# The opening of a two-layer encoder: order of the first loads, PSUM banks for two blocks of x, idle products, place of the squares, and a new table of places

## Chip, core and metric

The kernel runs on one core of one Trainium2 chip. The metric is the device time of one execution in microseconds (us). Within a core, TensorE (PE; its weight loads are shown apart as PEld), VectorE (DVE), ScalarE (ACT), GpSimd (POOL) and SyncE (SP) each run their own queue of instructions in order and wait for each other through semaphores. [...]

## What is computed

Two layers of an encoder on x, 256 rows of 1024 columns, in float32. Each layer has a mixer (three kinds of attention side by side) and a channel part:

```python
for l in range(DEPTH):
    x = mixer_sublayer(x, ...)       # rms_norm, h @ w_in, three attentions, rms_norm each, @ w_out, + x
    x = channel_sublayer(x, ...)     # rms_norm, @ w_gate_up, conv over rows, gelu(g) * u, @ w_down, + x
```

For the opening, this is what matters: the first thing computed is `rms_norm(x, norm1_g[0]) @ w_in[0]`, with `w_in[0]` 1024 by 2560. The kernel multiplies by the gain `norm1_g` first, leaves the division by the root mean square for later, and so needs the sums of the squares of x only where the first results are used.

## The kernel before

**Products in three.** Every operand is split into a large and a small part (`hi`, `lo`), and a product of full precision is three matmuls: hi by hi, hi by lo, lo by hi (`mm3`, line 708). The `hi` of weights is made by an ACT copy and the `lo` by a DVE subtraction, piece by piece (`split`, lines 676 to 695); for the first two units of weights a piece is one block of 128 rows by 384 columns.

**Units of weights.** The weights come in units of up to 1 MB into four raw buffers, and are split into two pairs of `hi` and `lo` buffers. A unit of the first projection is four blocks of 128 rows by 384 columns; the first projection, `dq`, takes unit 0 (blocks 0 to 3 of x) and unit 1 (blocks 4 to 7), for two halves of the rows, t = 0 and 1: 24 matmuls per unit. `dk` takes units 2 and 3, `dv` units 4 and 5, and so on.

**Opening.** `START` (line 45) lists the first transfers by queue: x in five pieces (a pair is first block and number of blocks), the gains `g`, the identity `ident`, and the four blocks `w` of unit 0. `LANDS` (line 52) has the time, in ns, at which the planner takes each of them to have landed. `split_T` (line 722) transposes x on PE, block by block: two blocks, each for t = 0 and 1, share one PSUM tile of a bank; ACT then writes `hi`, times the gain, into hT, and DVE the `lo`. `mean_squares` (line 746) has ACT square x in four pieces (two halves of the columns, two of the rows) with sums; POOL makes the root mean square of them. Before all that, PE runs idle products on a tile of ones (`warm`, `WARM` and `WARM_MORE`, lines 577 to 590): 13 of them at their place, and 15 more with a rank 1000 later, which the planner puts wherever PE would otherwise have nothing to do.

**Order.** No engine's order is written by hand. The program is first recorded as a list of operations (`Plan.add`), numbered as they come, and then put in order by a planner (`Plan.order`, line 323): at every step it takes the operation that can start first by its own costs (`cost`, line 475), its due times and its free buffers; among those that can start at the same time, the one with the smallest rank. A rank is the operation's number, plus what `later` adds, plus an entry of the table `PLACES` (line 229), by number. PSUM counts as one region for a whole bank (`footprint`, line 137), so a reader of one half waits for the writers of the other. `nc.behind` names an operation that must come first; it is a further dependency of what is recorded while it is set.

The attention's chain, which the steps touch: dq's and dk's sums of squares on ACT, their root on POOL (`small_ms`, `small_rstd`), scaling and rotation on DVE (`act_z`, `act_sw`), transposes on PE. POOL also repeats the bias table (`na_repeat`, line 829: `act_nab<-act_few`). Projections are the work that PE does beside that (`Weave`).

Of the kernel before, what the change touches and what calls it, by code (L numbers as in the profile page):

```python
# [11 lines left out]
F32 = mybir.dt.float32  # L12
F32R = mybir.dt.float32r
I32 = mybir.dt.int32
AF = mybir.ActivationFunctionType
# [29 lines left out]
START = [  # L45
    ("act", "x", (0, 1)), ("sync", "g", 0), ("act", "x", (1, 1)), ("sync", "ident", 0), ("sync", "w", 0),
    ("sync", "w", 1), ("sync", "x", (2, 2)), ("sync", "w", 2), ("sync", "w", 3), ("sync", "x", (4, 2)),
# [3 lines left out]

LANDS = (4100, 3300, 5300, 3450, 5800, 6450, 7250, 8200, 8900, 9800, 10700, 10750, 10800)


WARM, WARM_MORE, WARM_W = 13, 15, 256

# [168 lines left out]
def handover(a, b):  # L225
# [3 lines left out]
PLACES = {  # L229
# [6 lines left out]
}  # L236
# [281 lines left out]
def encoder_kernel(  # L518
# [102 lines left out]
    views = [v for l in range(DEPTH) for v in units_of(l)]  # L621
    raws, parts, taken = [], [], [0]

# [52 lines left out]
    def split(i):  # L676
# [13 lines left out]
        for c in range(0, n if i not in kept else 0, h):  # L690
            e = min(c + h, n)
            nc.scalar.copy(hi[:, c:e], raw[:, c:e])
            nc.vector.tensor_tensor(lo[:, c:e], raw[:, c:e], hi[:, c:e].bitcast(F32), op=ALU.subtract)
        r = lambda z: z[:, :n].rearrange("p (a b) -> p a b", b=b)
# [27 lines left out]
    def split_T(srcs, hi, lo, k0, g, name):  # L722


        n = g.shape[1]
        for b in range(0, n, 2):
            m = min(2, n - b)
            ps = psw.tile([P, 2, S], F32, tag="w", name=f"pt_{name}_{b}")
            for i in range(m):
                k = b + i  # L730
                for t in range(NT):
                    nc.tensor.transpose(
                        ps[:, i, t * P : (t + 1) * P], srcs[t][:, k * P : (k + 1) * P], ident
                    )
            for i in range(m):
                k = b + i
                h, o = hi[:, k0 + k], lo[:, k0 + k]
                nc.scalar.activation(h, ps[:, i], AF.Copy, scale=g[:, k : k + 1])
                nc.vector.scalar_tensor_tensor(
                    o, ps[:, i], g[:, k : k + 1], h.bitcast(F32), ALU.mult, ALU.subtract  # L740
                )
# [4 lines left out]
    def mean_squares(name):  # L746

        ss = small.tile([P, NT, 2], F32, tag="ssx", name=f"ssx_{name}", bufs=2)
        for h in range(2):
            for t in range(NT):  # L750
                junk = act.tile([P, 512], F32, tag="s2k", name=f"sq_{name}{t}{h}", bufs=NS2K)
                nc.scalar.activation(
                    junk, xs[:, t, h * 512 : (h + 1) * 512], AF.Square, accum_out=ss[:, t, h : h + 1]
                )
        s1 = small.tile([P, NT], F32, tag="s1x", name=f"s1_{name}", bufs=2)
        nc.gpsimd.tensor_tensor(s1, ss[:, :, 0], ss[:, :, 1], op=ALU.add)
# [795 lines left out]
```

## Time and profile before

| | us |
|---|---|
| median of three runs | 608.26 (607.88 to 608.92) |
| profiled execution | 608.41 |
| its span | 606.6 |
| PE busy in the span | 600.9 |
| ACT busy | 428.6 |
| DVE busy | 484.9 |

The span runs from the first to the last instruction that the profile shows; what lies around it is the start and the end of the program. Almost all instructions are issued through one line, 472, so the profile's groups are told apart by tiles: `const_warm` is the idle products, `const_x` x, `wp_raw`, `wp_hi` and `wp_lo` the weights as loaded and split, `act_hT` the transposed x, `act_s2k` among others the squares, `psa_a` and `psw_w` PSUM. In a timeline, a row has the start, the time (of all instructions of the row, where an xcount is over 1), the engine, what is written and read, and in brackets the idle time of the engine before it with what ended it. Matmuls are pipelined, so the distance of their starts says more than their durations.

### The profile page before, as it was taken

The page shows a single profiled execution, that of the slowest core. Times are in us where ns is not written, and L with a number is a line of the kernel's source. Part 1 is how long each engine was busy: PE and PEld are TensorE (multiplying, and loading weights), DVE is VectorE, ACT ScalarE, POOL GpSimd, SP SyncE. Part 2 cuts the span into 40 slices and gives each one's busy share as a digit, 9 for nine tenths or more (in the row PEclk, how much of TensorE's full clock was granted, in tenths as well). Part 3 has the DMA queues.
Part 4 walks back from the last instruction along what each step waited for, and adds up shares of the span by engine and source line. Part 5 has one row for each costly group of instructions (what it writes and reads, how often), then busy time and mean ns, then how long its engine had stood idle before and what let it go on. Part 6 is the DMA issues. An engine that isn't in the chain of part 4 may idle for free.

```text
span 606.6 us, 9899 instructions
## 1 busy us (share of the span) xinstructions
PE 600.9 (99%) x3496; PEld 526.7 (87%) x3496; DVE 484.9 (80%) x995; ACT 428.6 (71%) x1065; POOL 80.9 (13%) x130
## 2 busy tenths in 40 slices
PE   8999999999999999999999999999999999999997
PEld 7999898888888888888899989888888888888886
DVE  4899897997788988887777898777977777777775
ACT  6889999686666767666688899676765555665661
POOL 2733030103400000000022214421000000000000
PEclk9999999999999999999999999999999999999999
DMA  8994303566598899988455726844465555555601
GB/s 280 296 294 140 105 36 107 195 202 228 185 224 297 278 342 322 318 304 290 153 147 162 248 70 243 291 163 139 142 205 209 174 175 206 184 166 207 199 9 69
DMA packets 85217, 121.44 MB, mean 200 GB/s; under 512 B 9880, under 2 KB 69880, under 8 KB 85168
## 3 DMA queue, kind: packets, MB, share of 16 engines
q1 hardware_dynamic: 82896, 112.17, 56.3%
q0 software_dynamic: 1728, 8.39, 3.9%
q8 instruction: 27, 0.44, 0.3%
q10 hardware_dynamic: 544, 0.26, 0.2%
q14 instruction: 22, 0.18, 0.1%
HBM read 110.93 MB, written 9.88 MB: 199 GB/s over the span
## 4 chain that ended last, share of the span: by engine, by line
PE 96%; ACT 2%; DVE 1%; POOL 0%; issue 0%; DVEq 0%; ACTq 0%; POOLq 0%
PE psw_w L472 53%; PE psa_a L472 43%; ACT act_s2k L472 1%; ACT wp_hi L472 0%; DVE act_z L472 0%; DVE wp_lo L472 0%; POOL small_rstd L472 0%; ACT act_z L472 0%; ACT act_hT L472 0%; DVE act_sw L472 0%; POOL small_ms L472 0%; DVE const_x L472 0%; DVE act_qo L472 0%; POOL const_warm L472 0%; DVEq L472 0%
## 5 line engine op out<-in xcount | busy, mean ns | idle before, releaser
L472 DVE TENSOR_TENSOR wp_lo<-wp_raw,wp_hi 128x512 fp32r<-128x512 f32 (+2 forms) x332 | 231.5, 731 | 59.1 <-ACT wp_hi L472 39.3
L472 ACT CAST wp_hi<-wp_raw 128x512 fp32r<-128x512 f32 (+2 forms) x332 | 203.0, 663 | 22.8 <-PE psw_w L472 10.2
L472 PE MATMUL psw_w<-act_hT,wp_hi 128*128 128x512 f32 x704 | 180.4, 393 | 0.0
L472 PEld LDWEIGHTS psw_w<-act_hT,wp_hi 128*128 128x128 f32 x704 | 127.8, 189 | 24.8 <-DVE act_hT L472 0.7
L472 PE MATMUL psa_a<-wp_hi,act_hT 128*128 128x384 f32 (+2 forms) x448 | 113.1, 333 | 0.7 <-ACT wp_hi L472 0.7
L472 PEld LDWEIGHTS psw_w<-act_hT,wp_lo 128*128 128x128 f32 x704 | 97.7, 190 | 6.8
L472 PE MATMUL psw_w<-act_hT,wp_lo 128*128 128x256 f32 x704 | 102.2, 282 | 0.0
L472 PEld LDWEIGHTS psa_a<-wp_hi,act_hT 128*128 128x128 f32 x448 | 78.3, 189 | 3.4 <-ACT wp_hi L472 0.9
L472 ACT COPY act_s2k<-psw_w 128x256 f32<-128x256 f32 x88 | 32.4, 373 | 62.2 <-PE psw_w L472 61.9
L472 PE MATMUL psa_a<-wp_lo,act_hT 128*128 128x384 f32 (+2 forms) x224 | 74.4, 334 | 0.1
L472 PE MATMUL psa_a<-wp_lo,act_ch 128*128 128x512 f32 (+1 forms) x176 | 68.9, 392 | 0.0
L472 PE MATMUL psa_a<-wp_hi,act_ch 128*128 128x512 f32 x176 | 68.8, 392 | 0.0
L472 PE MATMUL psa_a<-wp_hi,act_cl 128*128 128x512 f32 (+1 forms) x176 | 68.5, 393 | 0.0
L472 DVE TENSOR_TENSOR act_s2k<-psw_w,act_s2k 128x256 f32<-128x256 f32 x88 | 36.6, 421 | 14.5 <-ACT act_s2k L472 14.1
L472 PEld LDWEIGHTS psa_a<-wp_lo,act_hT 128*128 128x128 f32 x224 | 42.2, 189 | 2.4 <-DVE wp_lo L472 1.0
L472 PEld LDWEIGHTS psa_a<-wp_hi,act_cl 128*128 128x128 f32 x176 | 33.1, 188 | 7.5
L472 PEld LDWEIGHTS psa_a<-wp_hi,act_ch 128*128 128x128 f32 x176 | 33.2, 189 | 6.7
L472 PEld LDWEIGHTS psa_a<-wp_lo,act_ch 128*128 128x128 f32 x176 | 33.1, 188 | 6.7
L472 DVE SCALAR_TENSOR_TENSOR act_s2k<-act_s2k,act_cw,act_s2k 128x255 f32<-128x255 f32 x88 | 36.7, 477 | 1.4 <-ACT act_s2k L472 1.3
L472 ACT ACTIVATE act_s2k<-act_s2k 128x512 f32<-128x512 f32 x22 | 13.9, 631 | 30.2 <-DVE act_s2k L472 30.2
L472 ACT ACTIVATE act_s2k<-act_s2k,act_cw 128x256 f32<-128x256 f32 x44 | 24.1, 595 | 15.3 <-DVE act_s2k L472 15.3
L472 POOL TENSOR_TENSOR small_rstd<-small_ms,const_mh 128x6 f32<-128x6 f32 (+2 forms) x26 | 30.8, 1186 | 14.4 <-DVE small_ms L472 12.8
(132 smaller groups left out, 791.6 us busy)
## 6 DMA issues: line engine op xcount, KB each, us to landing
wp_raw<-in_w_gate_up_dram SPq DMA_DIRECT2D x44, 1024.0 KB, 5.1
wp_raw<-in_w_down_dram SPq DMA_DIRECT2D x22, 1024.0 KB, 7.3
wp_raw<-in_w_in_dram SPq DMA_DIRECT2D x14, 768.0 KB, 6.0
wp_raw<-in_w_in_dram SPq DMA_DIRECT2D x8, 1024.0 KB, 9.1
wp_raw<-in_w_out_dram SPq DMA_DIRECT2D x8, 768.0 KB, 8.4
dram_khi<-act_mixT_hi SPq DMA_DIRECT2D x4, 768.0 KB, 3.6
dram_klo<-act_mixT_lo SPq DMA_DIRECT2D x4, 768.0 KB, 8.3
wp_lo<-dram_klo POOLq DMA_DIRECT2D x4, 768.0 KB, 4.8
```

The source lines that it names most:

```text
L472: getattr(o.engine.real, o.method)(*map(real, o.args), **{k: real(v) for k, v in o.kw.items()})
```

## The change

- **Loads.** Unit 0's first block of weights goes on ACT's queue as its second transfer, and x's second block goes on SP's queue in its place. `LANDS` is set anew.
- **A bank each.** Blocks 0 and 1 of x in layer 0 (`ALONE`) get a PSUM tile each instead of sharing one.
- **Idle products.** `WARM_MORE` is 7 instead of 15.
- **Squares.** In layer 0 the squares of x's first half of the columns (`HELD`) depend on the last ACT cast of unit 0.
- **Other order.** `PLACES` has 75 entries instead of 56. As there are eight idle products fewer, number n of the new table is number n + 8 of the old. So read, 47 entries are the same, nine old ones are gone and 28 are new. Seventeen of the new ones lie between the new numbers 67 and 320: later by some 100 are one transpose of x's block 5, the evacuation of block 7 and the last square; earlier are the first two casts of unit 1 (85 and 87), the transpose of the other gains (158), four of dq's sums of squares with POOL's two steps behind them (181 to 187) and POOL's repeat of the bias table (300); one of dk's scalings (274) is later, and three PE instructions move by 20 to 83. The other eleven new ones are casts of weights, a scaling, a square and five up-projection matmuls in later stages of both layers.

```diff
 START = [
-    ("act", "x", (0, 1)), ("sync", "g", 0), ("act", "x", (1, 1)), ("sync", "ident", 0), ("sync", "w", 0),
+    ("act", "x", (0, 1)), ("sync", "g", 0), ("act", "w", 0), ("sync", "ident", 0), ("sync", "x", (1, 1)),
     ("sync", "w", 1), ("sync", "x", (2, 2)), ("sync", "w", 2), ("sync", "w", 3), ("sync", "x", (4, 2)),
...
-LANDS = (4100, 3300, 5300, 3450, 5800, 6450, 7250, 8200, 8900, 9800, 10700, 10750, 10800)
+LANDS = (4100, 3300, 4800, 3800, 5200, 5900, 6900, 7700, 8500, 9400, 10400, 10500, 10600)
+ALONE = ("n100",)
+HELD = (("n10", 0),)
-WARM, WARM_MORE, WARM_W = 13, 15, 256
+WARM, WARM_MORE, WARM_W = 13, 7, 256
...
 PLACES = {
+    67: 104, 79: 101, 85: -246, 87: -158, 117: 90, 158: -74, 181: -210, 182: -210, 184: -212, 185: -212, 186: -212,
+    187: -212, 237: 20, 274: 315, 300: -116, 315: 83, 320: 49, 520: -53, 542: 173, 583: -96, 586: 125, 608: -286,
...
             nc.scalar.copy(hi[:, c:e], raw[:, c:e])
+            if i == 0:
+                split_at[:] = [len(nc.ops) - 1]
...
-            ps = psw.tile([P, 2, S], F32, tag="w", name=f"pt_{name}_{b}")
+            if name in ALONE and b == 0:
+                ps = [psw.tile([P, S], F32, tag="w", name=f"pt_{name}_{i}") for i in range(m)]
+            else:
+                both = psw.tile([P, 2, S], F32, tag="w", name=f"pt_{name}_{b}")
+                ps = [both[:, i] for i in range(m)]
...
         for h in range(2):
+            nc.behind = split_at[0] if (name, h) in HELD else None
             for t in range(NT):
                 junk = act.tile([P, 512], F32, tag="s2k", name=f"sq_{name}{t}{h}", bufs=NS2K)
...
+        nc.behind = None
```

More of the change, by code (lines that the diff above doesn't have):

```diff
@@ L621, in encoder_kernel @@
     views = [v for l in range(DEPTH) for v in units_of(l)]
-    raws, parts, taken = [], [], [0]
+    raws, parts, taken, split_at = [], [], [0], []
     PER_LAYER = len(views) // DEPTH
@@ L732, in split_T @@
                     nc.tensor.transpose(
-                        ps[:, i, t * P : (t + 1) * P], srcs[t][:, k * P : (k + 1) * P], ident
+                        ps[i][:, t * P : (t + 1) * P], srcs[t][:, k * P : (k + 1) * P], ident
                     )
@@ L737, in split_T @@
                 h, o = hi[:, k0 + k], lo[:, k0 + k]
-                nc.scalar.activation(h, ps[:, i], AF.Copy, scale=g[:, k : k + 1])
+                nc.scalar.activation(h, ps[i], AF.Copy, scale=g[:, k : k + 1])
                 nc.vector.scalar_tensor_tensor(
-                    o, ps[:, i], g[:, k : k + 1], h.bitcast(F32), ALU.mult, ALU.subtract
+                    o, ps[i], g[:, k : k + 1], h.bitcast(F32), ALU.mult, ALU.subtract
                 )
```

12 rows, old and new, of the table PLACES are left out of this document.

## Prediction

> **What bounds the kernel now.** I read the page first: the busy times, then the chain that ended last.
>
> ```profile
> span 606.6 us, 9899 instructions
> PE 600.9 (99%) x3496; PEld 526.7 (87%) x3496; DVE 484.9 (80%) x995; ACT 428.6 (71%) x1065; POOL 80.9 (13%) x130
> PE 96%; ACT 2%; DVE 1%; POOL 0%; issue 0%; DVEq 0%; ACTq 0%; POOLq 0%
> ```
>
> TensorE (PE) is busy 600.9 of 606.6 us and carries 96% of the chain. The change takes no real product away, only eight idle ones, so it can win time only where PE waits, or runs idle products, for want of data. The waits of PE after 15 us, by what ended them, and the stages of the first 120 us, say where that is.
>
> ```profile
> PEld psw_w L472 <- issue: 1.4, 5, 0.4
> PEld psa_a L472 <- DVE wp_lo L472: 0.7, 2, 0.4
> PEld psw_w L472 <- ACT wp_hi L472: 0.7, 2, 0.4
> PEld psw_w L472 <- DVE act_hT L472: 0.7, 3, 0.4
> PEld psw_w L472 <- DVE wp_lo L472: 0.2, 1, 0.2
> ```
> ```profile
> 7.30:14.16 6.86, 6.17 (x40) 5.58 (x39) 5.11 (x13) 6.74 (x20) 0.29 (x2) 1.00 1.03 358
> ...
> 20.00:35.00 15.00, 14.90 (x89) 14.55 (x88) 13.24 (x32) 12.54 (x56) 14.26 (x23) 1.00 0.96 287
> 35.00:60.00 25.00, 25.00 (x180) 23.80 (x180) 24.18 (x69) 22.03 (x77) 5.77 (x10) 1.00 0.74 211
> 60.00:120.00 60.00, 60.00 (x413) 52.30 (x412) 53.48 (x136) 52.30 (x144) 10.77 (x14) 1.00 0.32 105
> ```
>
> The columns of the second fence are the stretch, its length, the busy time of PE, PEld, DVE, ACT and POOL, granted clock, DMA share and GB/s. After 15 us PE has little to win: its weight loads wait 3.7 us in all, in 13 pieces. From 7.30 to 14.16 it is ScalarE (ACT) that is full, 6.74 of 6.86 us. So the opening bounds itself: PE starts late and then waits for ACT. The opening on PE, then on ACT:
>
> ```profile
> 0.98 3.17 PE L472 MATMUL psw_w<-const_warm 128*128 128x256 bf16 x14 [0.98 <-POOL const_warm L472]
> ...
> 4.70 0.63 PE L472 MATMUL psw_w<-const_ident,const_x 128*128 128x128 f32 x2
> 5.13 1.27 PE L472 MATMUL psw_w<-const_warm 128*128 128x256 bf16 x5
> 6.19 0.54 PE L472 MATMUL psw_w<-const_ident,const_x 128*128 128x128 f32 x2
> ...
> 7.30 0.44 PE L472 MATMUL psa_a<-wp_hi,act_hT 128*128 128x384 f32 x1
> ...
> 14.16 0.61 PE L472 MATMUL psa_a<-wp_hi,act_hT 128*128 128x384 f32 x2 [0.69 <-ACT wp_hi L472]
> ```
> ```profile
> 5.66 0.51 ACT L472 CAST wp_hi<-wp_raw 128x384 fp32r<-128x384 f32 x1 [2.64 <-DMA wp_raw<-in_w_in_dram]
> 6.77 0.48 ACT L472 ACTIVATE act_hT<-psw_w,const_gains 128x256 fp32r<-128x256 f32 x1 [0.60 <-DVE wp_lo L472]
> 7.14 0.50 ACT L472 CAST wp_hi<-wp_raw 128x384 fp32r<-128x384 f32 x1
> 7.54 0.63 ACT L472 ACTIVATE act_s2k<-const_x 128x512 f32<-128x512 f32 x1
> ...
> 8.17 0.46 ACT L472 ACTIVATE act_hT<-psw_w,const_gains 128x256 fp32r<-128x256 f32 x1
> ...
> 12.26 0.83 ACT L472 ACTIVATE act_hT<-psw_w,const_gains 128x256 fp32r<-128x256 f32 x2
> ...
> 12.98 0.64 ACT L472 ACTIVATE act_s2k<-const_x 128x512 f32<-128x512 f32 x1
> ...
> 13.59 3.41 ACT L472 CAST wp_hi<-wp_raw 128x384 fp32r<-128x384 f32 x8
> ```
>
> x's first block is transposed at 4.70 to 5.33, its second at 6.19 to 6.73. ACT evacuates the first (act_hT) only at 6.77, because both share one PSUM bank, which the planner treats as one region. The first product follows at 7.30. The second unit's first product stands at 14.16, 0.69 us late, because its cast stands behind the last square of x on ACT: 12.98, then 13.59.
>
> **The change part by part.**
> *A bank for each of two blocks.* ACT can evacuate block 0 when its own transposes end, 4.70 + 0.63 = 5.33, instead of 6.77. One more PSUM buffer of four is held for a while; at this point only the idle products and the gains hold others, so I cost it at nothing.
>
> *First weights on ACT's queue, x's second block on SyncE's (SP).* Each DMA takes the other's place, so no issue is added and the bytes ahead of the third transfer are the same. How early the weights land is not shown. The ends are the landing of the one transfer ahead of them on ACT's queue and today's cast:
>
> ```profile
> const_x<-in_x_dram ACTq DMA_DIRECT2D x1, 128.0 KB, 2.3
> ```
>
> Issued at 0.72, x's first block landed at 0.72 + 2.3 = 3.0; today's weights let ACT go at 5.66. I take 4.9, nearer to 5.66, since another block of x competes with them. Little hangs on it. ACT needs 0.37 (6.77 to 7.14) for block 0 and about 0.5 for the cast, so with 5.33 as the start both are done at 6.2; with weights at 5.66 only at 6.3. What then stands ahead of the first product is PE's own order: x's second block is due (LANDS 5200) before that product, so its two transposes go first and PE is free at about 6.4 (today 6.57). **First product: 7.30 to 6.4, a lead of 0.9.**
>
> *Fewer idle products.* 28 become 20. Of today's 28, 27 run before 7.30, in time in which PE has no data; removing them wins nothing by itself, beyond letting the two transposes go some 0.2 earlier, which is in the 6.4.
>
> *Squares of x later.* Four squares stand on ACT between 7.54 and 13.59, 0.63 each (7.54 to 8.17) and 0.61 (12.98 to 13.59). The first two now wait for the fourth cast of unit 0, and by the new places the first two casts of unit 1 go ahead of ready squares. ACT's work up to unit 1's first cast, without squares, is 4 casts at 0.40 (7.14 to 7.54) and 8 evacuations at 0.36 (12.26 to 12.98 for two): 4.5 us, or 5.33 + 4.5 = 9.8. Unit 1 isn't there yet:
>
> ```profile
> wp_raw<-in_w_in_dram SPq DMA_DIRECT2D x1, 384.0 KB, 4.6
> ```
> ```profile
> 6.28 2.06 SPq L472 DMA_DIRECT2D wp_raw<-in_w_in_dram  x4
> ```
>
> Issued at 6.28 and 4.6 us under way, its first half landed at 10.9. The cast and the handover make 10.9 + 0.5 + 0.1 = 11.5 for the earliest product of unit 1 as far as ACT goes, and 1.1 us is left on ACT for one or two squares meanwhile. Behind the waiting squares nothing is queued by the hold itself; the planner puts other work ahead. Who waits for them is POOL:
>
> ```profile
> 15.32 0.40 POOL L472 TENSOR_SCALAR small_he<-small_mex 128x2 f32<-128x2 f32 x1
> 18.68 0.29 POOL L472 TENSOR_SCALAR small_ms<-small_ss,small_he 128x6 f32<-128x6 f32 x1 [2.97 <-ACT act_s2k L472]
> ```
>
> Their sum is ready 3 us before its first use, so a delay by two squares (1.25 us) is covered; without that cover each would cost 0.6.
>
> PE has to do, between its first product and unit 1, 24 products and the 12 transposes left:
>
> ```profile
> 15.39:20.08 4.69, 4.69 (x28) 1.00 1.03 310
> ```
>
> 28 products in 4.69 us are 0.17 each, so 4.1; the transposes 1.2 at about 0.1, other small things 0.2: 5.5. PE comes to unit 1 at 6.4 + 5.5 = 11.9, after ACT's 11.5. **Lead at this point: 14.16 - 11.9 = 2.2.** Above that nothing is to be had: PE would be without a gap from 6.4 on.
>
> *How much of 2.2 survives.* ACT's and DVE's work isn't less, it is reordered. ACT ends unit 1's casts and all squares at about 5.33 + 4.5 + 2.5 (squares) + 1.6 (four casts) + 0.6 (waits for x and weights) = 14.5, against 13.59 + 4 x 0.41 = 15.2 today: ACT's own lead is 0.7. What it lacks it must take from idle time later, which exists:
>
> ```profile
> 23.42 1.76 ACT L472 CAST wp_hi<-wp_raw 128x384 fp32r<-128x384 f32 x4 [1.96 <-DMA wp_raw<-in_w_in_dram]
> ```
>
> ACT sits idle 1.96 us before 23.42. With dk's product done 2 us sooner, its squares can fill that gap. Between 35 and 120 us DVE is busy 77.7 of 85 us and ACT 74.3, so neither stops a lead of 1 to 2 us but neither gives it freely. Bounds for what is kept: 0.7 (ACT's lead) and 2.2. I take the middle, **1.5**.
>
> *Other order.* Seventeen new places lie in the opening and first projections (their part is in the sum above), eleven in later stages, and nine old ones go. What they can win there is bounded by the 3.7 us of waits after 15 us, most of them pieces of 0.2 to 0.4 that weight loads ahead of time hide; what they can lose no row shows, and I bound it by one such piece. I take 0.1 gained, between -0.4 and +0.4.
>
> Sum: 1.5 + 0.1 = 1.6. The profiled execution took 608.41 us, the span 606.6 and 1.8 around it, which stays; it lies 0.15 above the median, 608.26. **Forecast 608.41 - 1.6 = 606.8.**
>
> **The rivals.**
> *ACT's lead only.* DVE and ACT keep their order and PE's lead above 0.7 turns into waits near 34 us, where it waits for wp_lo even now. For it speaks ACT's 6.74 of 6.86; against, the 1.96 idle. Time: 608.41 - 0.7 = 607.7.
>
> *Transfers pace it.* The cast at 23.42 waits for weights, and the DMA share is 1.03 and 0.96 in the stages shown above up to 35 us, so that landing can't move. If all behind it holds its time, only the wait near 34 is saved: 608.41 - 0.3 = 608.1. Against it: PE reaches those weights, three units of 24 products at 0.17 after 14.16, only at 26.4, so a lead of 2 us still finds them.
>
> *PE's slow rate lasts.* Idle products come every 0.21 us until 6.19 (five from 5.13 to 6.19) and faster later:
>
> ```profile
> 6.57 0.82 PE L472 MATMUL psw_w<-const_warm 128*128 128x256 bf16 x6
> ```
>
> six until 7.30 are 0.12 each, though the granted clock reads 1.00 throughout. So PE needed 5.4 us of unbroken work (0.98 to 6.4) for full speed. With 20 idle products there may be a gap before the first product. If the slow rate lasts until about 10, 3.4 us of products run at half speed and 1.7 is lost: 608.5. [...] Against it: PE stays busy to within some tenths of the first product.
>
> *Slower: POOL's copy in the way.* The new places move the 2.16 us copy of the bias table ahead of dk's statistics on POOL, which is busy 14.26 of 15 us in 20 to 35:
>
> ```profile
> 24.12 2.16 POOL L472 COPY act_nab<-act_few 28x1984 f32<-28x1984 f32 x1
> ...
> 26.58 0.89 POOL L472 TENSOR_SCALAR small_ms<-small_ss,small_he 128x6 f32<-128x6 f32 x1 [0.29 <-ACT act_s2k L472]
> ```
>
> Today it ends 0.3 before dk's statistics can start. If it begins less than 2.16 before they could, the whole dk chain is late by up to 2.16, and with ACT's lead alone the time is 608.41 - 0.7 + 2.16 = 609.9. It decides once that delay exceeds PE's lead. Against it: the copy needs only its own small load, and dq's statistics are moved ahead of it.
>
> **How the numbers follow.** Forecast 0.55 (606.2 to 607.1); all 2.2 and the later waits kept, 605.9, 0.06; ACT's lead only 0.17; transfers 0.10; slow rate 0.05; POOL 0.07. 0.2% is 1.2 us, about what a measurement of this kernel can tell from no change; from the median that puts "faster" below 607.05. Faster: 0.55 + 0.06 and 0.03 of the ACT case, whose lead may be larger, 0.64; same 0.29; slower 0.07. The range 605.7 to 608.5 leaves out the slower case and the tails.
>
> **What the profile after would show.** Right: ACT's first evacuation at about 5.4, ahead of the second block's transposes; first product near 6.4; unit 1's first product near 12 with no ACT wait before it; squares between unit 0's and unit 1's casts; a PE wait near 33 of not much over 0.4. Wrong: a first product after 7 (weights or order), products at twice their interval (clock), a new PE wait on wp_lo or act_z of 1 us or more between 20 and 40 (lead given back), or dk's statistics behind act_nab on POOL.

## The result and the profile after

The changed kernel takes 610.38 us (median of 18 runs, 608.68 to 611.41); the kernel before took 608.49 on the same chips (18 runs, 607.88 to 609.52). The ratio is 1.0029, interval 1.0023 to 1.0036: 0.3% **slower**, 1.9 us, where 606.8 was forecast. The profiled execution took 610.58 with a span of 608.8.

The page of the kernel after, busy times and the chain that ended last:

```profile
span 608.8 us, 9884 instructions
PE 601.8 (99%) x3488; PEld 526.5 (86%) x3488; DVE 485.3 (80%) x995; ACT 428.2 (70%) x1065; POOL 83.2 (14%) x130
PE 94%; DVE 4%; ACT 1%; POOL 1%; issue 0%; POOLq 0%; DVEq 0%; ACTq 0%
```

PE is as busy as before, and its share of the chain fell from 96 to 94%, to DVE's gain. Something besides PE has come onto the path. The timeline of ACT in the opening, after:

```profile
4.99 1.28 ACT L480 ACT_TABLE_LOAD   x1 [4.99 <-DVE const_gains L480]
6.29 0.47 ACT L480 ACTIVATE act_hT<-psw_w,const_gains 128x256 fp32r<-128x256 f32 x1
6.66 0.50 ACT L480 CAST wp_hi<-wp_raw 128x384 fp32r<-128x384 f32 x1
...
10.66 0.84 ACT L480 ACTIVATE act_hT<-psw_w,const_gains 128x256 fp32r<-128x256 f32 x2 [2.03 <-PE psw_w L480]
```

And one row of the same timeline before:

```profile
1.74 1.28 ACT L472 ACT_TABLE_LOAD   x1 [1.74 <-issue]
```

In both profiles ACT loads a function table (`ACT_TABLE_LOAD`, 1.28 us) ahead of its first instruction that computes. Before, that was a cast that waits for a transfer, and the table load ran at 1.74, when nobody needed ACT. After, the first is an evacuation, which needs the gains from DVE and the transposes from PE, and the wait for DVE stands ahead of the table load. It runs at 4.99, and block 0 is evacuated at 6.29. PE in the opening, after:

```profile
4.90 0.60 PE L480 MATMUL psw_w<-const_warm 128*128 128x256 bf16 x4
5.34 0.38 PE L480 MATMUL psw_w<-const_ident,const_x 128*128 128x128 f32 x2
7.21 0.62 PE L480 MATMUL psa_a<-wp_hi,act_hT 128*128 128x384 f32 x2 [1.49 <-ACT wp_hi L480]
7.81 0.69 PE L480 MATMUL psa_a<-wp_lo,act_hT 128*128 128x384 f32 x1
8.29 0.52 PE L480 MATMUL psa_a<-wp_hi,act_hT 128*128 128x384 f32 x1
8.61 0.52 PE L480 MATMUL psa_a<-wp_lo,act_hT 128*128 128x384 f32 x1
```

The weights came early, and x's second block is transposed at 5.34 instead of 6.19: the loads do what they should. Then PE stands still for 1.49 us until 7.21, with no idle products left to run. The products that follow are 0.32 apart instead of 0.17, and the granted clock (the last but two of the columns) says why. It is 0.50 between 8.5 and 11.0, and in stretches of 5 us:

```profile
5.00:10.00 5.00, 3.51 (x17) 2.84 (x16) 2.38 (x5) 3.44 (x6) 0.00 (x0) 0.78 0.96 322
10.00:15.00 5.00, 5.00 (x30) 4.73 (x30) 2.04 (x6) 4.33 (x13) 0.00 (x0) 0.88 1.05 372
15.00:20.00 5.00, 5.00 (x29) 4.79 (x29) 4.95 (x11) 5.00 (x20) 2.41 (x6) 1.00 1.00 299
```

The first product of unit 1 stands at 14.99, 0.8 us later than before. More is lost behind that. What PE and its weight loads waited for from 15 to 60 us, after:

```profile
PE psw_w L480 <- ACT act_s2k L480: 0.8, 1, 0.8
...
PEld psa_a L480 <- DVE wp_lo L480: 1.3, 4, 0.4
PEld psw_w L480 <- ACT act_s2k L480: 1.0, 1, 1.0
PEld psa_a L480 <- DVE act_z L480: 0.4, 1, 0.4
PEld psw_w L480 <- ACT wp_hi L480: 0.2, 1, 0.2
```

The wait of 0.8 to 1.0 us stands at 53 us and is new, as are small ones at 28, 30 and 38. The first product of the FFN, a mark behind both, in before and after:

```profile
120.14 0.50 PE L472 MATMUL psw_w<-act_hT,wp_hi 128*128 128x512 f32 x1
```
```profile
122.96 0.50 PE L480 MATMUL psw_w<-act_hT,wp_hi 128*128 128x512 f32 x1
```

It is 2.8 us late; what follows gives 0.6 of that back, and the span is 2.2 us longer. So there are two questions: what the opening lost, and what PE lost between unit 1 and the FFN.

### The profile page after: what moved, and what is told of

The parts are those of the page before. It is cut to its first block, busy times and chain, and to the rows that moved or that the text cites. A ratio compares the mean times of both kernels' runs of the same rounds, so it can differ in the third digit from the quotient of the medians.

```text
span 608.8 us, 9884 instructions
## 1 busy us (share of the span) xinstructions
PE 601.8 (99%) x3488; PEld 526.5 (86%) x3488; DVE 485.3 (80%) x995; ACT 428.2 (70%) x1065; POOL 83.2 (14%) x130
## 4 chain that ended last, share of the span: by engine, by line
PE 94%; DVE 4%; ACT 1%; POOL 1%; issue 0%; POOLq 0%; DVEq 0%; ACTq 0%
PE psw_w L480 52%; PE psa_a L480 42%; DVE wp_lo L480 2%; DVE act_z L480 1%; DVE act_sw L480 0%; POOL small_ms L480 0%; POOL small_rstd L480 0%; ACT L480 0%; DVE const_v L480 0%; ACT act_z L480 0%; DVE act_ko L480 0%; ACT act_qo L480 0%; ACT wp_hi L480 0%; DVE act_nab L480 0%; ACT act_s2k L480 0%
## 5 line engine op out<-in xcount | busy, mean ns | idle before, releaser
L480 PE MATMUL psa_a<-wp_hi,act_ch 128*128 128x512 f32 (+1 forms) x176 | 68.9, 392 | 0.0
```

Of the source, the lines that this page charges most:

```text
L480: getattr(o.engine.real, o.method)(*map(real, o.args), **{k: real(v) for k, v in o.kw.items()})
```

## The experiments

Sixteen kernels ran, one of them twice (e13 and e16). "Unit 1" is the start of unit 1's first product, "FFN" that of the FFN's first, both from the one profiled execution; "between" is their difference. Ratios are against the kernel before, run in the same rounds, with their intervals. A wait of PE that is given below with the time at which it begins is the distance between the starts of two products, less the usual 0.17.

How far marks of single executions scatter, three kernels with the same opening and order up to small moves show: before, e9 and e14 have unit 1 at 13.99 to 14.20 and the FFN at 119.95 to 120.14. An execution can also lie far off its kernel's median. e10's profiled one took 610.67, 2.3 us over the median; that excess lies behind the FFN, from where it takes 488.8 us to the end, against 486.5 before.

| kernel | median, us | ratio | unit 1 | FFN | between |
|---|---|---|---|---|---|
| before | 608.49 | 1 | 14.16 | 120.14 | 105.98 |
| after | 610.38 | 1.0029 [1.0023, 1.0036] | 14.99 | 122.96 | 107.97 |
| e1 early table | 608.42 | 1.0001 [0.9993, 1.0010] | 12.68 | 121.61 | 108.93 |
| e2 PE filled | 609.88 | 1.0023 [1.0014, 1.0031] | 13.51 | 121.66 | 108.15 |
| e4 bank alone | 608.41 | 0.9998 [0.9989, 1.0006] | 14.04 | 120.74 | 106.70 |
| e5 old places | 612.71 | 1.0063 [1.0048, 1.0079] | 15.17 | 123.91 | 108.74 |
| e6 sums in one | 609.11 | 1.0014 [1.0005, 1.0023] | 12.63 | 120.79 | 108.16 |
| e7 copy behind tables | 609.07 | 1.0012 [1.0003, 1.0021] | 12.74 | 121.09 | 108.35 |
| e8 cast first, both | 608.74 | 1.0007 [0.9997, 1.0017] | 12.63 | 120.11 | 107.48 |
| e9 before, sums apart | 608.49 | 1.0001 [0.9992, 1.0010] | 13.99 | 119.95 | 105.96 |
| e10 new opening, old order | 608.35 | 0.9998 [0.9989, 1.0007] | 12.61 | 120.15 | 107.54 |
| e11 old opening, new order | 609.92 | 1.0022 [1.0013, 1.0031] | 14.19 | 122.13 | 107.94 |
| e12 lo9 later | 608.95 | 1.0002 [0.9993, 1.0011] | 12.64 | 120.89 | 108.25 |
| e13 copy on ACT | 607.99 | 0.9987 [0.9978, 0.9995] | see e16 | see e16 | |
| e14 before, copy on ACT | 608.52 | 1.0000 [0.9990, 1.0010] | 14.20 | 119.95 | 105.75 |
| e15 short squares | 608.34 | 0.9995 [0.9986, 1.0004] | 12.55 | 119.57 | 107.02 |
| e16 copy on ACT again | 608.45 | 0.9988 [0.9978, 0.9997] | 12.83 | 120.42 | 107.59 |
| e17 late table, old order | 609.60 | 1.0013 [1.0004, 1.0021] | 13.09 | 120.32 | 107.23 |
| e18 new order, copy on ACT | 608.37 | 0.9999 [0.9990, 1.0008] | 12.61 | 120.42 | 107.81 |

### The opening: table load, clock, bank

**e1.** One column is copied on ACT ahead of its first operation, so that the table load belongs to an instruction without a wait.

```diff
             for i in self.order():
                 o = self.ops[i]
+                if o.engine.name == "ACT" and o.method != "dma_start" and self.first_act:
+                    out, src = self.first_act
+                    self.scalar.real.copy(out.bind(), src[:, :1].bind())
+                    self.first_act = None
```

> The changed kernel with one more instruction: a one-column ACT copy ahead of ACT's first evacuation, so that the load of ACT's function table (1.28 us) no longer stands behind the wait for the gains; nothing else is reordered. Theory A (the table load on the path opens a wait on PE, in which its rate falls): the table load at about 1.7, first product near 6.1 instead of 7.21, no products at half rate, unit 1 near 12, time 606.5 to 607.3. Rival B (the new places after the opening cost about 2 us by themselves): first product as early, but the waits between 28 and 54 us stay and the time is 608.5 to 609.5.

Timeline of ACT in e1:

```profile
1.74 1.28 ACT L482 ACT_TABLE_LOAD   x1 [1.74 <-issue]
3.03 0.19 ACT L482 COPY const_fo<-const_mh 128x1 f32<-128x1 f32 x1
4.99 0.47 ACT L492 ACTIVATE act_hT<-psw_w,const_gains 128x256 fp32r<-128x256 f32 x1 [1.76 <-PE psw_w L492]
```

The evacuation is at 4.99, the first product at 5.91, unit 1 at 12.68, 1.5 us ahead of before. The time falls by 2.0 us against after, to that of the kernel before. So the table load is shown to be the loss of the opening; but a lead of 1.5 us is not worth 1.5 us. The time is just below the rival's range, and the waits that the rival named have stayed. The second question is what remained.

**e2.** The changed kernel with 16 more idle products ahead of the first product; the table load stays late.

```diff
+                if o.method == "matmul" and self.first_product and o.args[0].tile is not self.first_product[1].tile:
+                    n, ps, one = self.first_product
+                    for _ in range(n):
+                        self.tensor.real.matmul(ps.rearrange(...), one.bind(), ..., start=True, stop=True)
+                    self.first_product = None
```

> The changed kernel with 16 more idle products between the second block's transposes and the first real product, so that PE doesn't stand idle there; the table load stays on the path. Theory A: first product still near 7.2, but products at 0.17 instead of 0.32 between 7 and 11; the part of the loss that the rate makes goes, about 1.2 of 2: 608.6 to 609.3. If the rate doesn't matter (ACT alone is late): 610 and over, no change from the changed kernel.

The first product stays at 7.27, the granted clock reads 1.00 from 5 us on, and unit 1 comes at 13.51, 1.5 us earlier than in after. The median is 0.5 us lower, but the intervals of e2 and after overlap. The executions of after point the same way: in 8 of the 18 the mean granted clock is 0.996 or 0.997, with a median of 610.63, and in the other ten 0.999 or 1.000, with 609.99. So in after a low clock follows PE's idle 1.5 us (0.78 from 5 to 10 us), and most of what it cost at unit 1 is not in the end time.

**e4.** The kernel before with the bank each alone.

```diff
+            if name in ALONE and b == 0:
+                ps = [psw.tile([P, S], F32, tag="w", name=f"pt_{name}_{i}") for i in range(m)]
```

> The kernel before with one part of the change, a PSUM bank each for blocks 0 and 1. Theory A: an evacuation becomes ACT's first instruction, the table load goes behind the wait for the gains (start near 4.7 instead of 1.7) and the first product comes at 6.9 to 7.3, no earlier than in the kernel before; time 608.3 to 610. Without theory A (the bank alone lets ACT start at 5.3): first product near 6.4 and time 607.3 to 608.

Its table load runs at 4.48, its first evacuation at 5.77 instead of 6.77, and the first product at 6.74. Unit 1 stays at 14.04, since ACT is full until then: it is busy 9.64 of the 10 us from 5 to 15, and PE waits 0.70 for its cast. No gain and no loss.

**e5.** The changed kernel with the old table of places, every number less 8.

```diff
-PLACES = {67: 104, 79: 101, 85: -246, ...}
+PLACES = {367: -35, 480: 15, 520: -53, ...}
```

> The changed kernel with the table of places of the kernel before, renumbered; the table load stays on the path. Theory A: no faster than the changed kernel, 610 to 611.5. Rival B (the new places are the loss): back to 608 to 609.

It is 2.3 us slower than after. Places that were set for one stream of times don't fit another: the old table is not the old order. Part of it is the clock again: in four of its six executions the mean granted clock is 0.994 to 0.997, with a median of 613.45, against 611.18 in the other two. So this run can't tell what the new order costs; e10 and e11 do.

### What PE lost behind the opening: two pairs of engines

In e1 three rows stood out, two on POOL, one on DVE (the first of the two shown):

```profile
23.87 1.98 POOL L492 COPY act_nab<-act_few 28x1984 f32<-28x1984 f32 x1
...
45.12 1.99 POOL L492 TENSOR_SCALAR small_ms<-small_ss,small_he 128x6 f32<-128x6 f32 x1 [8.08 <-DVE wp_lo L492]
```
```profile
24.12 2.14 DVE L492 TENSOR_TENSOR wp_lo<-wp_raw,wp_hi 128x384 fp32r<-128x384 f32 x1
27.08 0.55 DVE L492 TENSOR_TENSOR wp_lo<-wp_raw,wp_hi 128x384 fp32r<-128x384 f32 x1
```

The same subtraction takes 0.55 us at 27.08 and 2.14 beside POOL's copy; PE waits 0.59 us for it at 25.55. The wait at 51 goes back to the reverse: POOL's `small_ms` takes 1.99 us at 45.12 (0.57 before, at 44.95) beside a run of DVE instructions. Theory P: the two engines hold each other up, and the new order puts such pairs on the path. Theory L: the statistics are late because the squares are. These runs move single instructions in the finished order and leave all else:

```diff
-            for i in self.order():
+            for i in moved(self.order()):
```

**e6** moves the second and third sum into `act_nab` (720, 721) directly behind the first, **e7** POOL's copy (300) with its store (301) behind the tables, as they stood before; both on top of e1.

> The changed kernel with the early one-column copy (table load off the path, as in e1), and in the finished order two instructions moved on VectorE alone: the second and third sum of the mask into act_nab stand right behind the first, ahead of the four products wp_lo of unit 8, as in the kernel before. In e1 these two (44.95, 1.42 us) run beside GpSimd's small_ms (45.12), which takes 1.99 us there against 0.57 before; small_rstd is late by that, VectorE waits 1.27 us for it and PE 1.0 us at 51.45. Theory P (the two engines hold each other up: while one of these VectorE instructions runs, GpSimd's stands): small_ms of cq takes under 0.7, PE's wait at 51 to 53 falls under 0.2, and the end comes 0.8 to 1.0 earlier than e1: ratio 0.998 to 0.9987 against before. Theory L (the statistics are late because the opening's squares are late, and the place of the sums is nothing): small_ms stays long or the wait is still there, ratio as e1, 0.9995 to 1.0005.

> The changed kernel with the early one-column copy, and in the finished order one move on GpSimd: the copy of act_nab (2.0 us) stands behind the tables act_cdk and act_sdk, as in the kernel before, and its store behind it. In e1 it runs at 23.87 and VectorE's wp_lo at 24.12 takes 2.14 us instead of 0.55; PE waits 0.59 for it at 25.55. Theory P: that wp_lo takes 0.55 again, another VectorE instruction that begins at 25.0 to 27.0 takes about 2, the wait of 0.59 goes, and the end is 0.2 to 0.6 earlier than e1: ratio 0.999 to 0.9997. Theory L: the wait at 25.55 stays, whatever GpSimd does there, and the ratio is as e1's, 0.9995 to 1.0005.

Neither gained. In e6, POOL and DVE:

```profile
44.30 1.99 POOL L502 TENSOR_SCALAR small_ms<-small_ss,small_he 128x6 f32<-128x6 f32 x1 [8.08 <-ACT act_s2k L502]
```
```profile
43.06 3.09 DVE L502 TENSOR_TENSOR wp_lo<-wp_raw,wp_hi 128x512 fp32r<-128x512 f32 x5
46.07 0.41 DVE L502 CUSTOM_DVE_ANT_0 act_s2k<-psw_w,const_dil 128x256 f32<-128x256 f32 x1
```

The sums are gone from there, and beside five `wp_lo` subtractions `small_ms` takes just as long, 1.99 us: it ends at 46.29, when the run of five has ended (46.15). My expectation took the wrong instruction for the cause. In e7 the wait of 0.59 goes, as expected, but waits of 0.3 us at 26.7 and 28.3 are left, and the time doesn't show it.

**e9**, the reverse, puts the sums apart in the kernel before.

```diff
+MOVES = ((728, 'behind', 443), (729, 'behind', 728))
```

> The reverse: the kernel before, with one thing of the new order put into its finished order: the second and third sum into act_nab stand behind the four products wp_lo of unit 8, where the changed kernel has them. Theory P: they run at about 45 beside GpSimd's small_ms of cq, which takes about 2 us instead of 0.57, PE gets a wait of 0.7 to 1.0 us near 51 to 52, and the end is 0.7 to 1.0 later than before: ratio 1.0011 to 1.0017. Theory L: nothing of this, ratio 0.9996 to 1.0004.

No difference: `small_ms` takes 0.57 at 44.76. The place of the sums as such is not the cause. DVE's run, here with the sums at its end, is over at 45.19 and `small_ms` at 45.33.

**e8** has no added copy; the first cast stands ahead of the first evacuation on ACT, which frees the table load too, and both moves are made. **e12** also moves the fifth `wp_lo` (584) behind two softmax sums; its last entry is the only difference.

```diff
+MOVES = ((41, 'ahead', 53), (720, 'behind', 719), (721, 'behind', 720), (300, 'behind', 261), (301, 'behind', 300), (584, 'behind', 521))
```

> The changed kernel without the added copy; in its finished order the first cast of unit 0 stands ahead of the first evacuation on ACT (so the table load has no wait for VectorE ahead of it), and the moves of e6 and e7 are both made. Theory P with the table load: table load at about 1.7, first product at 5.9 to 6.0, unit 1's first product at 12.7, no wait over 0.3 us at 25 to 56, and the end 1.2 to 1.6 earlier than e1: 606.8 to 607.2 us, ratio 0.997 to 0.998, faster than before, near what was forecast. Rival: as soon as these waits go, PE runs into the next ones (transfers of the weights at 25 to 45, ACT) and the lead is lost there: 608.0 to 608.5, ratio 0.999 to 1.0005.

> e8 (first cast ahead on ACT, the sums into act_nab in one piece, the copy of act_nab behind the tables) with one more move on VectorE: the first product wp_lo of unit 9 stands behind the second softmax sum instead of ahead of the first. In e8 GpSimd's small_ms begins at 44.17 and takes 1.14 us (1.99 in e6 and e7), and ends when VectorE's unbroken run of products ends; with that product gone from the run, VectorE pauses earlier. Theory P (GpSimd's instruction stands until VectorE pauses): small_ms takes under 0.8 us, PE's wait at 50.5 (0.46 in e8) falls under 0.15, the end 0.3 to 0.5 earlier than e8's 608.74: ratio 0.9995 to 1.0003. Rival: small_ms is as long as in e8, or the wait stays: ratio as e8's, 1.0005 to 1.001.

The table load is free in both, unit 1 at 12.63. POOL and DVE in e8:

```profile
44.17 1.14 POOL L490 TENSOR_SCALAR small_ms<-small_ss,small_he 128x6 f32<-128x6 f32 x1 [8.07 <-ACT act_s2k L490]
```
```profile
43.36 3.09 DVE L490 TENSOR_TENSOR wp_lo<-wp_raw,wp_hi 128x512 fp32r<-128x512 f32 x5
```

Here `small_ms` ends at 45.31, while the run of five goes on to 46.45. So it does not always stand until DVE pauses, as e12 took it to. e8 is no faster than e1, and in e12 `small_ms` still takes 1.39 and PE still waits 1.0 at 50.75. Theory P names the right two engines, but these repairs move the wait rather than remove it. Theory L's reason was not shown by any of them.

### The order by itself

**e10** and **e11** cut the kernels apart. Each runs one kernel's order up to a point behind the last square of x, and the other kernel's order from there on; `ORDERED` lists the operations of the one opening and then all others in the other kernel's order. Only the order is fixed; the planner still gives out the buffers.

```diff
+ORDERED = [...]
...
+                    if i != wanted_of[e][-1]:
+                        continue
```

> The changed kernel's opening (loads, bank each, 7 fewer idle products, held squares; its own order of the first 147 instructions in the planner's count, that is up to the last square of x and the first casts of unit 2), with the first cast ahead of the first evacuation on ACT so that the table load has no wait for VectorE; every instruction behind these stands in the order of the kernel before. Theory O (the new order behind the opening gives the lead back): unit 1's first product at 12.6 to 12.8, no wait over 0.3 us at 25 to 56, first product of the FFN at 118.4 to 119.0 (before 120.14, after 122.96), and the end at 606.8 to 607.4: ratio 0.997 to 0.9985. Theory W (an earlier opening cannot be kept: what follows is paced by weights, ACT and VectorE, whatever the order): unit 1's first product at 12.7, but waits appear at 20 to 56 and the FFN begins at 119.8 to 120.4; 608.1 to 608.8, ratio 0.9993 to 1.0005.

> The reverse: the kernel before up to the first product of unit 2's casts (its own loads, banks, idle products and order), and every instruction behind it in the order of the changed kernel. Theory O: PE's wait of 0.5 to 1.0 us at 51 to 53 is there, with 0.2 to 0.3 us each near 27, 28 and 36; the FFN begins 1.2 to 2.0 later than before (121.3 to 122.1) and the end is 609.6 to 610.4: ratio 1.002 to 1.003. Theory W: as before, 608.2 to 608.8, ratio 0.9995 to 1.0005.

e11 answers one half: with the old opening the **new order alone costs 0.22%**, 1.4 us. The waits of after are there (PE and its weight loads, 15 to 60 us, e11):

```profile
PE psw_w L716 <- ACT act_s2k L716: 0.6, 1, 0.6
...
PEld psa_a L716 <- DVE wp_lo L716: 1.1, 3, 0.4
PEld psw_w L716 <- ACT act_s2k L716: 0.8, 1, 0.8
```

"Between" is 107.94 as in after, 2.0 more than before. e10 answers the other half against theory O: with the old order behind it, the new opening is worth **nothing**, though unit 1 starts 1.55 us early. "Between" grows by 1.56. So the lead is gone before the FFN. Against the same product of the kernel before (the order is the same), it is 1.36 us at 26.00 and 0.16 at 28.42. POOL, DVE and PE in e10:

```profile
18.76 0.29 POOL L723 TENSOR_SCALAR small_ms<-small_ss,small_he 128x6 f32<-128x6 f32 x1 [1.99 <-DMA const_gq<-in_q_norm_g_dram]
...
24.15 2.17 POOL L723 COPY act_nab<-act_few 28x1984 f32<-28x1984 f32 x1
```
```profile
24.53 1.97 DVE L723 TENSOR_TENSOR act_sw<-act_z,act_sdq 128x48 f32<-128x48 f32 x2
26.42 0.55 DVE L723 TENSOR_TENSOR wp_lo<-wp_raw,wp_hi 128x384 fp32r<-128x384 f32 x1
```
```profile
27.03 0.44 PE L723 MATMUL psa_a<-wp_lo,act_hT 128*128 128x384 f32 x1 [0.51 <-DVE wp_lo L723]
```

`small_ms` starts at 18.76, before at 18.68; POOL's copy at 24.15, before at 24.12. The chain of statistics stands where it stood. PE comes to unit 4's `wp_lo` 1.4 us earlier and meets DVE with an `act_sw` that takes 1.97 us beside POOL's copy; in the kernel before the copy was over in time.

### Why the lead isn't kept

**e13** and, for its profile, **e16**: e10 with layer 0's copy made by ACT, in an idle stretch ahead of unit 4's first cast. **e14** does the same to the kernel before. **e15** is e10 with short squares; it leaves most of each sum out, so its results are not the encoder's.

```diff
-        nc.gpsimd.tensor_copy(
+        (nc.scalar.copy if l == 0 else nc.gpsimd.tensor_copy)(
...
+                wide = 16 if name == "n10" else 512
-                    junk, xs[:, t, h * 512 : (h + 1) * 512], AF.Square, accum_out=ss[:, t, h : h + 1]
+                    junk[:, :wide], xs[:, t, h * 512 : h * 512 + wide], AF.Square, accum_out=ss[:, t, h : h + 1]
```

> e10 (the new opening, table load free, the old order behind it) with layer 0's copy into act_nab made by ACT instead of GpSimd, ahead of the first cast of unit 4, where ACT stands idle for 1.5 us in e10 (21.4 to 22.94). In e10 GpSimd's copy runs from 24.15 to 26.3, VectorE's act_sw at 24.53 takes 1.97 us instead of 0.32 beside it, wp_lo behind it comes at 26.42, and PE waits 0.68 us at 26.18 and 0.30 at 27.49. Theory P (the copy holds VectorE up, and that is where the lead goes): act_sw takes about 0.32, the waits at 26 to 28 fall to under 0.4 in sum, the FFN begins 0.6 to 1.0 earlier than in e10 (119.2 to 119.6) and the end is 607.4 to 607.8: ratio 0.998 to 0.999. Theory W (weights landing at 22.8 to 29 us, or the chain of statistics, take the lead anyway): other waits take their place, 608.1 to 608.6, ratio 0.9993 to 1.0003.

> The kernel before with the same one thing: layer 0's copy into act_nab on ACT, ahead of the first cast of unit 4 (ACT idle from 21.46 to 23.42 there). In the kernel before no wait of PE stands behind VectorE's 1.96 us at 24.51. Theory P: nothing to win here, ratio 0.9995 to 1.0005, so that what e13 wins over e10 is the kept lead. If the copy's place is worth something by itself, this kernel is faster too, by as much as e13 against e10.

> e10 with the four squares of layer 0's x cut from 512 columns to 16 (the sums of squares leave out the other columns): about 0.45 us less of ACT's time each, 1.8 us in all, ahead of dq's squares, which start at 17.24 in e10 and at 17.16 in before. Theory A (the statistics start no earlier because ACT's work ahead of them is no shorter): dq's squares at 15.5 to 16.2, GpSimd's small_ms 1 us earlier or more, PE's waits at 26 to 28 smaller, the end 0.5 to 1.2 us earlier than e10: ratio 0.9975 to 0.999. Theory T (transfers): dq's squares come earlier, but GpSimd waits for const_gq (landed at 18.63) and ACT for wp_raw, the chain from 19 us on stays as in e10: ratio 0.9993 to 1.0003.

> The same kernel as e13, for its profile. Theory P: act_sw at 24.5 takes about 0.32 instead of 1.97, PE's waits at 26 to 28 come to under 0.4 in all, the first product of the FFN stands at 119.2 to 119.6, and the time agrees with e13's: ratio 0.998 to 0.9995. Theory W: the waits are there as in e10 and e13's 0.13% was chance: ratio 0.9995 to 1.0005.

Both runs of the one kernel are faster than before, by 0.13 and 0.12% by the ratio, with intervals below 1, though e16's median is only 0.17 us lower (608.45 against 608.62 in its rounds). The same edit does nothing to the kernel before (1.0000). ACT, DVE and PE in e16:

```profile
21.21 1.85 ACT L723 COPY act_nab<-act_few 28x1984 f32<-28x1984 f32 x1
23.74 1.76 ACT L723 CAST wp_hi<-wp_raw 128x384 fp32r<-128x384 f32 x4 [0.68 <-DMA wp_raw<-in_w_in_dram]
```
```profile
24.76 0.32 DVE L723 TENSOR_TENSOR act_sw<-act_z,act_sdq 128x48 f32<-128x48 f32 x2
...
30.37 0.33 DVE L723 TENSOR_TENSOR act_sw<-act_z,act_sdk 128x48 f32<-128x48 f32 x2 [1.00 <-ACT act_z L723]
```
```profile
32.96 0.44 PE L723 MATMUL psa_a<-wp_lo,act_hT 128*128 128x384 f32 x1 [0.50 <-DVE wp_lo L723]
```

`act_sw` is back to 0.32 and no wait is left at 26 to 28: the copy is shown to be what held DVE there. PE keeps its lead of 1.1 us past this place (27.47 against 28.58 for the same transposes of `act_z`). But now it waits at 32 to 33 for another `wp_lo`; at 35 the lead is 0.2 (34.96 against 35.16), and the FFN starts at 120.42, no earlier than before, instead of the expected 119.2 to 119.6.

The rows say what sets that second place. Unit 4's cast waits for its weights until 23.74 (23.42 before). On ACT dk's squares stand behind it and start at 25.40 (25.13). POOL's `small_ms` of dk waits for them until 26.84 (26.58), DVE waits for the scaled dk until 30.37 (30.53), and the late `wp_lo` stands behind that on DVE, at 32.35. So by these rows the landing holds the chain to its old time; no run moved the landing to test it. Where the 0.12 to 0.13% come from is not shown either: the profiled execution of e16 took 608.68 and has none of the lead left at the FFN, and against e10 the intervals overlap.

e15 asked whether ACT's work ahead of dq's squares is the bound. ACT and POOL in e15:

```profile
15.06 1.75 ACT L723 CAST wp_hi<-wp_raw 128x384 fp32r<-128x384 f32 x4 [0.37 <-DMA wp_raw<-in_w_in_dram]
...
22.64 1.76 ACT L723 CAST wp_hi<-wp_raw 128x384 fp32r<-128x384 f32 x4 [1.71 <-DMA wp_raw<-in_w_in_dram]
```
```profile
18.24 0.29 POOL L723 TENSOR_SCALAR small_ms<-small_ss,small_he 128x6 f32<-128x6 f32 x1 [1.53 <-DMA const_gq<-in_q_norm_g_dram]
```

With 1.8 us less to do, ACT waits for weights instead, and `small_ms` comes 0.5 us earlier. In the profile all that follows is about 0.5 earlier than in e10, the FFN 0.6 (119.57), but the time is that of e10 within the intervals. That speaks for the transfers and against ACT's work.

**e17** is e10 with the table load late again (the evacuation ahead of the cast), **e18** the changed kernel with the cast first and the copy on ACT, in its own order.

The first cut is e17 against e10, the second e18 against after; dots stand for the rest of the list.

```diff
-... 17 40 18 41 53 19 37 20 51 ...
+... 17 40 18 53 19 37 20 41 51 ...
```
```diff
+... 17 40 18 41 53 19 ... 256 237 300 301 227 176 ...
...
-        nc.gpsimd.tensor_copy(
+        (nc.scalar.copy if l == 0 else nc.gpsimd.tensor_copy)(
```

> The changed kernel's opening as it is (first evacuation ahead of the first cast on ACT, so the table load stands behind the wait for VectorE's gains), and the old order behind it: e10 but for that one exchange. If the late table load costs by itself (1.3 us on ACT, PE idle 1.7 us, then the low clock): first product at 7.2, products 0.32 apart to 11, unit 1's first product at 15.0, the FFN 0.8 to 1.6 later than before, 609.2 to 610.0: ratio 1.0012 to 1.0025. If what comes behind the opening is paced by something else and takes it up: ratio 0.9995 to 1.0007.

> The changed kernel with its own order throughout, the first cast ahead of the first evacuation on ACT, and layer 0's copy into act_nab on ACT ahead of the first cast of unit 4 (ACT idle 1.6 us there in e1). If GpSimd's copy is what the new order loses by: no VectorE instruction of 2 us at 24 to 26, waits at 25 to 29 under 0.3 in all, 607.4 to 608.0, ratio 0.998 to 0.9993. If the new order loses behind that (PE's wait of 0.5 to 1.0 at 51, and 0.2 to 0.3 at 27, 28 and 36, are still there): as e8, 608.2 to 609.0, ratio 0.9995 to 1.001.

e17's ratio is 0.0015 above e10's: the late table load costs about 1 us with the old order too. PE idles 1.5 us again (the expectation's 1.7 was too long, it is 1.49 in both), but the clock stays up in its profile:

```profile
5.00:10.00 5.00, 3.51 (x22) 2.93 (x21) 2.42 (x6) 4.01 (x9) 0.00 (x0) 1.00 0.97 313
```

So this part of my expectation missed. In three of its twelve executions the mean granted clock is 0.997, with a median of 610.34; the other nine have 609.34, still 1.0 over e10. So the price of the late load is not the clock's alone. In e18 no instruction that DVE starts at 24 to 26 takes over 0.55 us, and still it is no faster than e1: PE waits 1.0 us at 50.25. The copy is not what the new order loses by.

## Why the prediction was wrong

Forecast and result lie 3.6 us apart (606.8 and 610.38). e1, the changed kernel with the table load out of the way, stands between them at 608.42. So 2.0 us are the table load, a term that the sum did not have, and 1.6 are the lead and the gain of the order, of which nothing is left even then.

- **"ACT can evacuate block 0 when its own transposes end, 5.33."** Failed. It ended the wait for the bank and overlooked the table load of 1.28 us, which in after stands ahead of ACT's first computing instruction and behind the wait for the gains (4.99): 6.29. With the load out of the way it is 4.99 (e1) and the first product, forecast at 6.4, comes at 5.91 and 6.34 (e1, e10) instead of 7.21. The working of that step held; one row of before, the table load at 1.74, was not looked at. It costs about 1 us with the old order (e10 to e17) and 2.0 with the new (e1 to after).
- **First weights at 4.9.** Right, if late: where the cast comes first it starts at 4.0 to 4.8 (e8 4.04, e16 4.27, e10 4.77).
- **"Removing them wins nothing by itself."** True, but they also covered a late first product. With fewer, PE stood idle for 1.49 us and its clock read 0.78 from 5 to 10 us in the profile of after; by the two groups of executions above that costs about 0.6 us, in fewer than half of them. The rival of the slow rate named products at half rate until about 10, and in after they are some 0.3 apart until 11. No run shows its price of 1.7 us: e2, without the gap, reaches unit 1 earlier by 1.48 us than after, and its median is 0.5 lower. The 5.4 us of unbroken work for full speed are one trace's: idle products are 0.11 apart from 4.90 in after, 3.9 us after PE's start, and 0.12 from 4.12 in e4, 3.1 us after it.
- **Unit 1 at 11.9, lead 2.2.** With a free table load 12.6 to 12.7, a lead of 1.5: from the first product to unit 1 it took 6.3 us in e10, not 5.5. The products and transposes took what the sum has for them; pauses of 0.1 to 0.25 us between them, which it left out, make the difference.
- **"How much of 2.2 survives ... I take the middle, 1.5."** Failed. None survives with the old order (e10: 1.36 us until 26, 0.16 at 28.4), and none up to the FFN in e16's profile with one copy moved. The step asked which engine is full, and found room; but the lead is lost to single meetings, first of DVE with POOL's copy, then of PE with a `wp_lo` that stands behind dk's statistics, which by e16's rows the landing of unit 4's weights holds to their old time. The number of the rival "Transfers pace it" (608.1) fits e10 (608.35), and its mechanism shows in e16. It was given 0.10 because PE reaches unit 4's weights only at 26.4, by when they have landed; but dk's squares wait on ACT behind the cast of these weights.
- **"Other order. I take 0.1 gained, between -0.4 and +0.4."** Failed with the old opening: 1.4 us lost (e11), most of it between unit 1 and 56 us. With the early opening the new order costs nothing against the old (e1 and e10). I bounded it by one wait of the kernel before. A new order makes waits that no row of the old one shows.
- **The slower rival** named POOL's copy and the right place, and gave 609.9; its mechanism was another. dk's statistics do come behind the copy, but what PE waits for is the `wp_lo` that DVE makes beside it, and that is not what the new order loses by (e18).

The terms don't simply add, as the medians by opening and order show (from several rounds, in which before's own median was 608.47 to 608.68):

| opening | old order | new order |
|---|---|---|
| old | 608.49 (before) | 609.92 (e11) |
| new, table load free | 608.35 (e10) | 608.42 (e1) |
| new, table load late | 609.60 (e17) | 610.38 (after) |

With the old order an early opening is worth nothing; with the new order it is worth 1.5 us, about what that order loses without it. So e1, e8, e10 and e18 all end near the kernel before. What sets PE's wait at 50 to 53 in the new order is shown only in part: GpSimd's `small_ms`, 1.99 us long beside DVE's run (e1, after), is one link, and no move took the wait away; it was shortest in e8, 0.4 us.

The best version is e13's: new opening, cast first, old order behind it, copy on ACT, 0.13% faster than before by the ratio and 0.4% faster than after.

## What to carry to other kernels

When an edit changes which instruction is an engine's first, look up what else hangs on the first one (here a 1.28 us table load) and put one without waits in front. A lead won at the start can be gone before the end (here 1.55 us at unit 1 in e10, none at the FFN); follow it stage by stage to a mark far behind before it is counted. To price a new order, run it alone, the old one elsewhere: a table of places moved to other numbers or times is not the old order (e5, 612.71).

## What the runs showed of the hardware

- A wait of ACT's first computing instruction can stand ahead of the table load: it starts at 4.99 in after and 4.48 in e4 instead of 1.74 in before, 1.28 us on the path.
- DVE and POOL instructions took longer side by side. `act_sw` took 1.97 us beside POOL's copy (e10) and 0.32 with the copy on ACT (e16); `wp_lo` took 2.14 beside it and 0.55 later (e1). `small_ms` took 1.99 beside DVE's run in e1 and 0.57 in before, where that run ends at 45.37 and `small_ms` at 45.52. In e6 POOL's instruction stood not for one but through the rest of a run of five; in e8 it took 1.14 and ended 1.14 before such a run did.
- After the same idle stretch of PE, 1.49 us, the granted clock fell to 0.78 in one profile (after, mean of 5 to 10 us) and stayed at 1.00 in another (e17). Executions of one kernel differ too: the mean clock was 0.997 or less in 8 of 18 of after and in 3 of 12 of e17. What decides it is open.
